# An encoder layer on one core: about 135 stores and loads move from SyncE's DMA queue to GpSimd's, and two gate norms change their chain

## The chip, the cores and the metric

The kernel runs on one core of one Trainium2 chip. The metric is device time in microseconds for one launch, median of several runs. The engines are named as the profile names them: PE (TensorE, matrix products), DVE (VectorE), ACT (ScalarE), POOL (GpSimd) and SP (SyncE, which here issues DMA transfers only). A transfer is issued by an instruction on the queue of one of these engines; it lands later, and whoever reads the data waits for its semaphore. DRAM stands for the chip's main memory.

## The reference, cut to what matters

One layer of a hybrid encoder, in fp32, for 1,024 prompt tokens of one stream and 64 sample tokens of another, model width 1,024:

```python
hn = rmsnorm(h, pre_mix_g)
z, xbc, dt, u_pool = split(hn @ w_in)               # 1,024 -> mixer widths
xbc = silu(causal_conv(xbc));  y, new_ssm = ssd_scan(xbc, softplus(dt))
y = (y + d_skip * xs) * silu(z)
y = grouped_rmsnorm(y, 2 groups) * ssm_norm_g       # the "gate norm"
pool = multiscale_causal_pool(u_pool)               # windows 2, 4, 8, 16
h = h + rmsnorm(concat(y, pool) @ w_out, post_mix_g)         # h1
f = (silu(hn2 @ w_gate) * (hn2 @ w_up)) @ w_down    # hn2 = rmsnorm(h1, pre_ffn_g)
h = h + rmsnorm(f, post_ffn_g)                      # h2
e = (p @ w_ple_proj) * sigmoid(h @ w_ple_gate)
y = h + rmsnorm(e, ple_norm_g)
```

Outputs are y for both groups and the new scan, convolution and pooling states.

## The kernel before

**Tiles.** Features lie on the 128 partitions, tokens along the free axis. The 1,088 tokens are four chunks of 272; the last chunk holds 208 prompt tokens and the 64 sample tokens. An fp32 product is made of three products of a shorter float format: each operand is split into a high half (a cast on ACT) and a low half (a subtraction in the helper `sub`, line 424, on DVE and at some places on POOL), and high x high, high x low and low x high are summed in PSUM.

**Stages.** Input projection and convolution; the scan in nine blocks; pooling; z gate and gate norm; output projection; post-mix norm with the residual x, whose result `h1` is stored to DRAM (`h1_d`); the FFN; and a last stage per chunk. The FFN uses a seven-product scheme over 2 x 2 blocks. It needs sums and differences of blocks, called forms. Forms of the FFN's input (`hq_d`) and of its inner activation (`af_d`) are stored to DRAM as they arise and loaded again later, by `al_...` and `ar_...` tiles, for the down product. The two stages overlap: while the last gate and up products run, the first down products start. Into gaps go the products of `p @ w_ple_proj`, whose result is stored to `e_d`.

**The last stage** (`post_ffn`, `post_ple`). For each chunk and each of four pairs of feature blocks, `two(i)` scales the FFN's result by `post_ffn_g` (ACT, two steps), multiplies it by the norm's factor, which PE has spread over the partitions (DVE, line 2566), adds the residual `h1`, which has been loaded into an `hr` tile (POOL line 2572 or DVE line 2575, by the pair), and splits the sum into the halves of `H2` (ACT line 2580, then `sub`). PE then multiplies by `w_ple_gate` (lines 521 and 504; its weights come as `raw_pg` and are split into `w_pg`, two of the eight low halves on POOL). `e_load` fetches a piece of the projection into an `el` tile. A tile's name in the profile is that of its buffer's first or last user, so an `hr` load can read `sq_f<-h_dram`, and an `el` load `sg<-e_dram`.

**Norm factors** (`rstd_job`, from line 526). PE sums squares over the partitions (line 539), DVE turns the sums into 1/sqrt on a small tile (`t_g` for gate norms), PE spreads it (line 548). There are two ways: ACT's reciprocal square root followed by three DVE steps (lines 582 to 591), open to some names once its table has been loaded, and a chain of nine DVE steps without ACT (lines 553 and 596 to 610).

**What sets the order.** The program is written by a planner, `Layout`. Jobs are generators that ask for an engine and a planned time; the planner keeps a clock for each engine and issues whatever can start first. The orders of PE, DVE, ACT and POOL are then fixed as written. `dma` (line 398) issues on a queue, SP's by default, and counts the same planned time whichever queue it is. Each queue issues in order: an instruction that waits holds what stands behind it. Transfers of a queue take turns on eight semaphores, so each also waits for the one eight before it. In the kernel before, one transfer goes through POOL's queue (the small load of `wdr` at the start) and 510 by SP's; POOL otherwise has 47 counted operations, mostly residual additions and low halves.

Of the kernel before, what the change touches and what calls it, by code (L numbers as in the profile page):

```python
# [7 lines left out]
F32 = mybir.dt.float32  # L8
# [12 lines left out]
CW = 272  # L21
# [320 lines left out]
def trunk(ctx, tc, xT, par, wmix, wdt, poolw, wout, wff, wdn, wpg, wpp, pT, ssm0,  # L342
# [63 lines left out]

    cp = const.tile([P, PWIDTH], F32, name="cp")
    scr = const.tile([P, 2], F32, name="scr")
    tabled, z_left = [False], [4 * NC]
# [115 lines left out]
    def rstd_job(accs, L, D, name, got, fast=False, rest=None, free=nts.give):  # L525
# [53 lines left out]

        if tabled[0] and (name[0] in "gmh" or name == f"f{ORD_E[0]}"):  # L580
            yield ("A", 0.2)
            ac.activation(y, v, AF.Abs_reciprocal_sqrt, scale=2.0 ** -24)
            if name == f"h{ORD_F[-1]}":
                tabled[0] = False
                ac.activation(scr[:, 0:1], ones[:, 0:1], AF.Silu)
            yield ("D", 0.16)
            ve.scalar_tensor_tensor(q, y, -(2.0 ** -37), y, ALU.mult, ALU.mult)
            yield ("D", 0.16, TW)
            ve.tensor_tensor(q, q, v, ALU.mult)
            yield ("D", 0.16, TW)  # L590
            ve.scalar_tensor_tensor(y, q, 1.5 * 2.0 ** -12, y, ALU.add, ALU.mult)
            yield from spread()
            return
# [560 lines left out]
    def ssd(c):  # L1154
# [89 lines left out]
        if c >= 7:  # L1244
            dma(ssm_o[:, c - 7], new, 512)
        if c + 1 < NSSD:
# [7 lines left out]
    def ssd_start():  # L1254
        yield lambda: bool(dt_done)
        spawn(decay(0), 2)
        yield lambda: 7 in conv_done
        yield ("S", 0, 1)
        dma(conv_o, conv_out, 48)
        spawn(ssd(0), 2)  # L1260
# [22 lines left out]
    def pool_post(gi):  # L1283
# [32 lines left out]
        for c, (t0, L) in enumerate(CH):  # L1316
# [15 lines left out]
            if M[c] is None:  # L1332
                yield ("S", 0, 0)
                dma(pool_d[c][:, gi], p_[:, :CH[c][1]], CH[c][1])
                spawn(give_later(nts, 4))
                spilled.append((c, gi))
            else:
                spawn(pool_split(c, gi, p_), 2)
# [3 lines left out]
        if len(pool_n) == 4:  # L1342
            exts.to_pages()
            dma(pool_o, pool_out, 120)

# [147 lines left out]
    def post_mix(c, mf, ss):  # L1493
# [7 lines left out]
        def two(i):  # L1501
# [21 lines left out]
            if XM[i] != "A":  # L1523
                n2.give(xr)
            at = dma(h1_d[c][:, 2 * i:2 * i + 2], v, 2 * L)
            ss2.add(v, lambda: spawn(scale(i, v, at), P_SCL))
# [126 lines left out]
    def qforms():  # L1653
# [20 lines left out]
        def form(f, src):  # L1674
# [7 lines left out]
            def low():  # L1682
# [4 lines left out]
                yield ("S", 0, 0)  # L1687
                Q_AT[f] = dma(hq_d[FORMS.index(f)], pg.bitcast(F32), 4 * CW)

# [404 lines left out]
    def whole_forms(q):  # L2094
# [3 lines left out]
        def store(f, t):  # L2098
            yield ("S", 0, 0)
            at[f] = dma(af_d[j][FORMS.index(f)].rearrange("p (c t) -> p c t", c=2), t, 2 * CW)  # L2100
            A_DONE[j, f] = 2
# [24 lines left out]
    def aforms(q):  # L2126
# [8 lines left out]
        def form(f, t):  # L2135
# [7 lines left out]
            def low():  # L2143
# [5 lines left out]
                for s in range(2):  # L2149
                    dma(dst[:, s, sl], v[:, s, sl].bitcast(F32), q.n * CW)  # L2150
                A_DONE[j, f] = A_DONE.get((j, f), 0) + q.n
# [61 lines left out]
    def proj_ready(c, m):  # L2213
        return lambda: c in p_done and f"pp{m // 4}" in W and len(banks.order) > 1

    def proj_group(c, m):
        def emit():
# [5 lines left out]
            def job():  # L2223
# [5 lines left out]
                yield ("S", 0, 0)  # L2229
                dma(e_d[c][:, m], e_, CW)  # L2230
                spawn(give_later(nts, 4), 5)
# [315 lines left out]
    def post_ffn(c, ss, prio):  # L2547
# [6 lines left out]
        def two(i):  # L2554
            v = fp2(c, i)
            for q in range(2):
                yield ("A", 0.5)
                ac.activation(v[:, q], v[:, q], AF.Identity, scale=pcol("post_ffn_g", 2 * i + q))
            if XF[i] != "A":
                yield n2.ok  # L2560
                hr = n2.take(f"hr{c}_{i}")
                yield ("S", 0, 0)
                at = dma(hr, h1_d[c][:, 2 * i:2 * i + 2], 2 * L)
            yield lambda: bool(flag)
# [103 lines left out]
    def e_load(c, i):  # L2668
        yield n2.ok
        e_ = n2.take(f"el{c}_{i}")  # L2670
        yield ("S", 0, 0)
        EL[c, i] = e_, dma(e_, e_d[c][:, 2 * i:2 * i + 2], 2 * CW)

# [213 lines left out]
```

## Time and profile before

| what | value |
|---|---|
| median of 3 runs | 1199.31 us (1197.8 to 1199.6) |
| the profiled execution | 1199.71 us, its span 1197.9 us |
| granted TensorE clock, mean | 0.995 |
| PE busy | 1182.2 us, 99% |
| DVE busy | 946.3 us, 79% |
| ACT busy | 619.3 us, 52% |
| POOL busy | 59.9 us, 5% |
| SP's queue (q1) | 176.56 MB, 43.7% of the 16 DMA engines |
| GpSimd's queue (q0) | 0.03 MB |

All times inside the execution are microseconds from the start of the span. Busy time of an engine says how much it did, not whether anyone waited for it; the list of waits says what PE stood still for, and the chain of waits names, step by step, what released the next piece of work.

### The profile page before, as it was taken

How to read it: one execution, taken by the hardware profiler on the slowest of the kernel's cores; microseconds unless marked ns; L12 is line 12 of the kernel's file. 1: busy time of each engine (PE TensorE's matmuls, PEld its weight loads, DVE VectorE, ACT ScalarE, POOL GpSimd, SP SyncE). 2: the span in 40 equal slices, each digit the busy share in tenths (PEclk: the TensorE clock that was granted, in tenths of full speed). 3: DMA queues.
4: the chain of work that ended last, by engine and by line, in shares of the span. 5: the costliest groups of instructions: out<-in, count | busy, mean ns of one | idle time of the engine just before them, and what ended most of it. 6: DMA issues, size and time to landing. Idle time of an engine off the chain costs nothing.

```text
span 1197.9 us, 23999 instructions
## 1 busy us (share of the span) xinstructions
PE 1182.2 (99%) x9547; PEld 1166.1 (97%) x9547; DVE 946.3 (79%) x1792; ACT 619.3 (52%) x1278; POOL 59.9 (5%) x48
## 2 busy tenths in 40 slices
PE   9999999999999999999999999999999999999997
PEld 7999999999999999999999999999999999999997
DVE  7697777875788797888888888888788688768855
ACT  7355657965668644444443344334554344347533
POOL 0000000111131000000000000000000000012301
PEclk9999999999999999999999999999999999999998
DMA  7022222143455224536546744677865254144422
GB/s 252 23 75 90 75 79 94 54 135 108 148 181 176 69 100 139 183 120 244 204 160 227 250 145 161 231 248 253 316 207 148 87 191 152 30 146 139 157 66 84
DMA packets 73380, 178.13 MB, mean 149 GB/s; under 512 B 8540, under 2 KB 16548, under 8 KB 73268
## 3 DMA queue, kind: packets, MB, share of 16 engines
q1 hardware_dynamic: 73092, 176.56, 43.7%
q8 instruction: 75, 1.23, 0.4%
q14 instruction: 37, 0.30, 0.1%
q0 software_dynamic: 32, 0.03, 0.0%
q10 hardware_dynamic: 144, 0.00, 0.0%
HBM read 131.50 MB, written 45.07 MB: 147 GB/s over the span
## 4 chain that ended last, share of the span: by engine, by line
PE 65%; DVE 2%; DMA 1%; issue 0%; DVEq 0%; SPq 0%; ACT 0%
PE psall L1921 47%; PE psall L2065 7%; PE psall L504 7%; PE psall L521 2%; DMA al_B<-af_dram 1%; DMA hr<-h_dram 0%; PE psall L539 0%; DVE E L2611 0%; DVE mixf L1550 0%; DVE mixf L1580 0%; DVE h_T L424 0%; PE psall L548 0%; DVE h L424 0%; DVE f L2338 0%; DVE f L2566 0%
## 5 line engine op out<-in xcount | busy, mean ns | idle before, releaser
L504 PE MATMUL psall<-x,w_in 128*128 128x272 f32 x1440 | 193.5, 290 | 0.0
L504 PEld LDWEIGHTS psall<-x,w_in 128*128 128x128 f32 x1440 | 183.9, 188 | 3.3 <-issue 2.8
L1921 PE MATMUL psall<-h_T,w_u_S 128*128 128x272 f32 x792 | 104.4, 288 | 0.0
L1921 PE MATMUL psall<-h_T,w_g_S 128*128 128x272 f32 x792 | 101.6, 288 | 0.2 <-DVE h_T L424 0.2
L1921 PEld LDWEIGHTS psall<-h_T,w_u_S 128*128 128x128 f32 x792 | 101.2, 188 | 0.0
L1921 PE MATMUL psall<-al_T,w_d_S 128*128 128x272 f32 x780 | 100.7, 288 | 0.0
L1921 PEld LDWEIGHTS psall<-h_T,w_g_S 128*128 128x128 f32 x792 | 100.1, 188 | 0.4 <-DVE h_T L424 0.4
L1921 PEld LDWEIGHTS psall<-al_T,w_d_S 128*128 128x128 f32 x780 | 98.9, 188 | 0.0
L504 PE MATMUL psall<-mix,w_out 128*128 128x272 f32 x720 | 93.3, 289 | 0.0
L504 PEld LDWEIGHTS psall<-mix,w_out 128*128 128x128 f32 x720 | 90.9, 188 | 0.0
L2338 DVE TENSOR_TENSOR f<-f,psall 128x544 f32<-128x544 f32 (+1 forms) x96 | 60.4, 636 | 32.7 <-PE psall L1921 32.1
L504 PE MATMUL psall<-h,w_pg 128*128 128x272 f32 x576 | 75.4, 290 | 0.0
L504 PEld LDWEIGHTS psall<-h,w_pg 128*128 128x128 f32 x576 | 73.0, 188 | 0.0
L1921 PE MATMUL psall<-al_B,w_d_A 128*128 128x272 f32 x528 | 71.1, 288 | 1.0 <-DMA al_B<-af_dram 1.0
L1921 PEld LDWEIGHTS psall<-al_B,w_d_A 128*128 128x128 f32 x528 | 68.1, 188 | 1.3 <-DMA al_B<-af_dram 1.3
L1802 ACT CAST w_d_S<-raw_d 128x384 fp32r<-128x384 f32 (+2 forms) x55 | 27.8, 530 | 58.0 <-DVE raw_d L1837 37.8
L424 POOL TENSOR_TENSOR w_pg<-raw_pg,w_pg 128x1024 fp32r<-128x1024 f32 x2 | 5.3, 2630 | 684.7 <-DVE f L2338 684.7
L1921 PE MATMUL psall<-h_B,w_g_A 128*128 128x272 f32 x288 | 38.3, 288 | 0.7 <-DVE sq_m L2082 0.7
L1921 PE MATMUL psall<-h_B,w_u_A 128*128 128x272 f32 x288 | 38.0, 288 | 0.0
L1921 PEld LDWEIGHTS psall<-h_B,w_g_A 128*128 128x128 f32 x288 | 36.9, 188 | 0.9 <-DVE sq_m L2082 0.9
L1921 PE MATMUL psall<-al_T,w_d_A 128*128 128x272 f32 x276 | 37.6, 289 | 0.0
L1921 PEld LDWEIGHTS psall<-h_B,w_u_A 128*128 128x128 f32 x288 | 36.8, 188 | 0.0
(559 smaller groups left out, 2488.1 us busy)
## 6 DMA issues: line engine op xcount, KB each, us to landing
hs_T<-hq_dram SPq DMA_DIRECT2D x28, 544.0 KB, 6.2
hs_B<-hq_dram SPq DMA_DIRECT2D x21, 544.0 KB, 5.7
raw_g<-in_wff_dram SPq DMA_DIRECT2D x22, 512.0 KB, 5.3
raw_u<-in_wff_dram SPq DMA_DIRECT2D x22, 512.0 KB, 4.5
raw_in<-in_wmix_dram SPq DMA_DIRECT2D x15, 512.0 KB, 3.7
af_dram<-sq_m SPq DMA_DIRECT2D x26, 272.0 KB, 5.2
ar_T<-af_dram SPq DMA_DIRECT2D x24, 272.0 KB, 3.4
raw_d<-in_wdn_dram SPq DMA_DIRECT2D x10, 512.0 KB, 4.3
```

Source lines behind the costliest of these rows:

```text
L424: eng.tensor_tensor(lo, src, hi.bitcast(F32), ALU.subtract)
L504: pe.matmul(out, lhsT, rhs, start=i == 0, stop=i == n - 1)
L521: pe.matmul(out, w.v(wi, k), act.v(xi, k, L), start=first and n == 0, stop=not left and n == 2)
L1802: ac.copy(v[:, 0], src)
L1921: pe.matmul(d[:, p - q.ps[0], :], w.v(wi, k), u.b(bf, xi, p, k), start=start and not k and not wi and not xi, stop=k == u.ks - 1 and wi == ...
L2065: pe.matmul(d, w.v(wi, k), b[:, xi, k, :], start=m in (1, 2, 5) and not k and not wi and not xi, stop=k == 1 and wi == 1, skip_group_check ...
L2338: ve.tensor_tensor(v[:, sl], v[:, sl], src[:, pl], ALU.add)
```

## The change

Constants name a queue for each kind of transfer. To GpSimd's queue go the stores of scan, convolution and pooling states (`ST_A`), of pooled pieces that are kept in DRAM (`ST_P`), of the forms (`ST_F`, for `hq_d` and `af_d`), and in the last stage the loads of the residual (`LD_H`) and of the projection (`LD_E`). Stores of `h1` and of the projection stay on SP (`ST_H`, `ST_E`). Gate norms lose ACT's way, so that all four chunks use the nine steps; of the four, the first two did so before, because the table was not loaded yet. Two more edits stand in the diff: the residual's load in `two` is issued ahead of the two scalings instead of behind them, and a projection group may start when one PSUM bank is free, where two were asked for. One line is inserted, so lines from 408 on are one higher in the changed kernel.

```diff
@@ -407,2 +407,3 @@
     cp = const.tile([P, PWIDTH], F32, name="cp")
+    ST_A, ST_P, ST_H, ST_F, ST_E, LD_H, LD_E = gp, gp, sy, gp, sy, gp, gp
     scr = const.tile([P, 2], F32, name="scr")
@@ -579,3 +580,3 @@
 
-        if tabled[0] and (name[0] in "gmh" or name == f"f{ORD_E[0]}"):
+        if tabled[0] and (name[0] in "mh" or name == f"f{ORD_E[0]}"):
             yield ("A", 0.2)
@@ -1244,3 +1245,3 @@
         if c >= 7:
-            dma(ssm_o[:, c - 7], new, 512)
+            dma(ssm_o[:, c - 7], new, 512, ST_A)
         if c + 1 < NSSD:
@@ -1258,3 +1259,3 @@
         yield ("S", 0, 1)
-        dma(conv_o, conv_out, 48)
+        dma(conv_o, conv_out, 48, ST_A)
         spawn(ssd(0), 2)
@@ -1333,3 +1334,3 @@
                 yield ("S", 0, 0)
-                dma(pool_d[c][:, gi], p_[:, :CH[c][1]], CH[c][1])
+                dma(pool_d[c][:, gi], p_[:, :CH[c][1]], CH[c][1], ST_P)
                 spawn(give_later(nts, 4))
@@ -1343,3 +1344,3 @@
             exts.to_pages()
-            dma(pool_o, pool_out, 120)
+            dma(pool_o, pool_out, 120, ST_A)
 
@@ -1524,3 +1525,3 @@
                 n2.give(xr)
-            at = dma(h1_d[c][:, 2 * i:2 * i + 2], v, 2 * L)
+            at = dma(h1_d[c][:, 2 * i:2 * i + 2], v, 2 * L, ST_H)
             ss2.add(v, lambda: spawn(scale(i, v, at), P_SCL))
@@ -1687,3 +1688,3 @@
                 yield ("S", 0, 0)
-                Q_AT[f] = dma(hq_d[FORMS.index(f)], pg.bitcast(F32), 4 * CW)
+                Q_AT[f] = dma(hq_d[FORMS.index(f)], pg.bitcast(F32), 4 * CW, ST_F)
 
@@ -2099,3 +2100,3 @@
             yield ("S", 0, 0)
-            at[f] = dma(af_d[j][FORMS.index(f)].rearrange("p (c t) -> p c t", c=2), t, 2 * CW)
+            at[f] = dma(af_d[j][FORMS.index(f)].rearrange("p (c t) -> p c t", c=2), t, 2 * CW, ST_F)
             A_DONE[j, f] = 2
@@ -2149,3 +2150,3 @@
                 for s in range(2):
-                    dma(dst[:, s, sl], v[:, s, sl].bitcast(F32), q.n * CW)
+                    dma(dst[:, s, sl], v[:, s, sl].bitcast(F32), q.n * CW, ST_F)
                 A_DONE[j, f] = A_DONE.get((j, f), 0) + q.n
@@ -2213,3 +2214,3 @@
     def proj_ready(c, m):
-        return lambda: c in p_done and f"pp{m // 4}" in W and len(banks.order) > 1
+        return lambda: c in p_done and f"pp{m // 4}" in W and banks.ok()
 
@@ -2229,3 +2230,3 @@
                 yield ("S", 0, 0)
-                dma(e_d[c][:, m], e_, CW)
+                dma(e_d[c][:, m], e_, CW, ST_E)
                 spawn(give_later(nts, 4), 5)
@@ -2555,5 +2556,2 @@
             v = fp2(c, i)
-            for q in range(2):
-                yield ("A", 0.5)
-                ac.activation(v[:, q], v[:, q], AF.Identity, scale=pcol("post_ffn_g", 2 * i + q))
             if XF[i] != "A":
@@ -2562,3 +2560,6 @@
                 yield ("S", 0, 0)
-                at = dma(hr, h1_d[c][:, 2 * i:2 * i + 2], 2 * L)
+                at = dma(hr, h1_d[c][:, 2 * i:2 * i + 2], 2 * L, LD_H)
+            for q in range(2):
+                yield ("A", 0.5)
+                ac.activation(v[:, q], v[:, q], AF.Identity, scale=pcol("post_ffn_g", 2 * i + q))
             yield lambda: bool(flag)
@@ -2671,3 +2672,3 @@
         yield ("S", 0, 0)
-        EL[c, i] = e_, dma(e_, e_d[c][:, 2 * i:2 * i + 2], 2 * CW)
+        EL[c, i] = e_, dma(e_, e_d[c][:, 2 * i:2 * i + 2], 2 * CW, LD_E)
 
```

SP has 322 rows where it had 457, POOL 169 where it had 52; PE has 4,579 for 4,582. Three places follow.

**The down product's first loads, on SP.** Before, with the stores of forms (`af_dram<-`) among the loads of forms (`al_...`):

```order
L399 DMA raw_d_0_1_9853<-in_wdn_dram 128x512
L399 DMA al_B_9891<-af_dram 128x1088
L399 DMA hs_T_9902<-hq_dram 128x1088
L399 DMA af_dram<-n_g_21_5485 128x544
L399 DMA al_B_9944<-af_dram 128x1088
L399 DMA al_B_9947<-af_dram 128x1088
L399 DMA al_T_9949<-af_dram 128x1088
L399 DMA al_T_9959<-af_dram 128x1088
L399 DMA af_dram<-p_3802 128x544
L399 DMA al_T_9968<-af_dram 128x1088
```

and with the change:

```order
L399 DMA raw_d_0_1_9861<-in_wdn_dram 128x512
L399 DMA al_B_9899<-af_dram 128x1088
L399 DMA hs_T_9910<-hq_dram 128x1088
L399 DMA al_B_9952<-af_dram 128x1088
L399 DMA al_B_9955<-af_dram 128x1088
L399 DMA al_T_9957<-af_dram 128x1088
L399 DMA al_T_9967<-af_dram 128x1088
L399 DMA al_T_9976<-af_dram 128x1088
L399 DMA al_T_10020<-af_dram 128x1088
```

The stores have left the row of loads; the two loads of `al_B` now stand straight behind the load of `hs_T`.

**The entry of the last stage.** SP before, with the four residual loads (`h_0_dram`) behind the loads of `raw_pg`:

```order
L399 DMA raw_pg_12495<-in_wpg_dram 128x1024
L399 DMA raw_pg_12555<-in_wpg_dram 128x1024
L399 DMA raw_pg_12598<-in_wpg_dram 128x1024
L399 DMA raw_pg_12633<-in_wpg_dram 128x1024
L399 DMA sq_f_12205<-h_0_dram 128x544
L399 DMA hr_1_12659<-h_0_dram 128x544 x2
L399 DMA sq_f_12610<-h_0_dram 128x544
L399 DMA raw_pg_12731<-in_wpg_dram 128x1024
L399 DMA raw_pg_12814<-in_wpg_dram 128x1024
```

and POOL with the change:

```order
L399 DMA af_dram<-n_g_21_5491 128x544
L399 DMA af_dram<-p_3810 128x544
L399 DMA af_dram<-sq_m_3274 128x544
L425 TENSOR_TENSOR w_pg_12615<-raw_pg_12566,w_pg_12614 128x1024
L399 DMA sq_f_12216<-h_0_dram 128x544
L399 DMA hr_1_12653<-h_0_dram 128x544 x2
L399 DMA hr_3_12668<-h_0_dram 128x544
L2573 TENSOR_TENSOR f_0_10455<-f_0_10455,sq_f_12216 128x2x272
L425 TENSOR_TENSOR w_pg_12626<-raw_pg_12609,w_pg_12625 128x1024
L2573 TENSOR_TENSOR f_0_10140<-f_0_10140,hr_1_12653 128x2x272
L399 DMA hr_3_12668<-e_dram 128x544
```

The four loads now stand behind the last store of forms and one low half of `w_pg`, and ahead of POOL's first addition; a second low half stands between the two additions.

**The gate norm of chunk 2 on DVE, then PE.** DVE before:

```order
L424 TENSOR_TENSOR w_out_3185<-raw_out_3182,w_out_3184 128x1024
L553 TENSOR_SCALAR t_g_3224<-psall 68x8
L424 TENSOR_TENSOR w_out_3209<-raw_out_3206,w_out_3208 128x1024
L587 SCALAR_TENSOR_TENSOR t_g_3224<-t_g_3224 68x8
L589 TENSOR_TENSOR t_g_3224<-t_g_3224 68x8
L591 SCALAR_TENSOR_TENSOR t_g_3224<-t_g_3224 68x8
L1416 SCALAR_TENSOR_TENSOR xs<-xs,cp,psall 128x272 x3
```

and with the change:

```order
L425 TENSOR_TENSOR w_out_3185<-raw_out_3182,w_out_3184 128x1024
L554 TENSOR_SCALAR t_g_3224<-psall 68x8
L597 TENSOR_SCALAR t_g_3224<-t_g_3224 68x8
L599 TENSOR_TENSOR t_g_3224<-t_g_3224 68x8
L601 TENSOR_TENSOR t_g_3224<-t_g_3224 68x8
L425 TENSOR_TENSOR w_out_3209<-raw_out_3206,w_out_3208 128x1024
L603 SCALAR_TENSOR_TENSOR t_g_3224<-t_g_3224 68x8
L605 SCALAR_TENSOR_TENSOR t_g_3224<-t_g_3224 68x8
L607 TENSOR_TENSOR t_g_3224<-t_g_3224 68x8
L609 SCALAR_TENSOR_TENSOR t_g_3224<-t_g_3224 68x8
L611 SCALAR_TENSOR_TENSOR t_g_3224<-t_g_3224 68x8
L1406 TENSOR_TENSOR acc_g_3_3246<-acc_g_3_3246,sq_g_3_3247 128x272
```

Three of the nine steps now stand ahead of a low half of `w_out`, five behind it, and an addition of squares for chunk 3 follows at once. PE before, around the spread of that factor:

```order
L504 MATMUL psall<-mix_00_2389,w_out_3169 128x272 x4
L504 MATMUL psall<-mix_01_2390,w_out_3169 128x272
L548 MATMUL psall<-cp,t_g_3224 128x68 x8
L504 MATMUL psall<-mix_01_2390,w_out_3169 128x272 x3
L504 MATMUL psall<-mix_00_2389,w_out_3184 128x272 x4
```

and with the change:

```order
L505 MATMUL psall<-mix_00_2389,w_out_3169 128x272 x4
L505 MATMUL psall<-mix_01_2390,w_out_3169 128x272 x4
L505 MATMUL psall<-mix_00_2389,w_out_3184 128x272 x3
L549 MATMUL psall<-cp,t_g_3224 128x68 x8
L505 MATMUL psall<-mix_00_2389,w_out_3184 128x272
```

The spread stands six products later. Chunk 3's sum and spread with the change:

```order
L540 MATMUL psall<-cp,acc_g_3_3312 68x1 x4
L505 MATMUL psall<-mix_00_2636,w_out_3072 128x272 x2
L505 MATMUL psall<-mix_01_2637,w_out_3072 128x272 x4
L505 MATMUL psall<-mix_00_2636,w_out_3119 128x272 x4
L505 MATMUL psall<-mix_01_2637,w_out_3119 128x272 x4
L505 MATMUL psall<-mix_10_2638,w_out_3119 128x272 x4
L549 MATMUL psall<-cp,t_g_3368 128x68 x8
```

Between the two stand 18 products; before, there were 15.

## The prediction

> **What bounds the kernel now.** I read the page's busy shares first, then the list of PE's waits, then the chain of waits and the timeline at the places which that list names. Busy share of each engine:
>
> ```profile
> PE 1182.2 (99%) x9547; PEld 1166.1 (97%) x9547; DVE 946.3 (79%) x1792; ACT 619.3 (52%) x1278; POOL 59.9 (5%) x48
> ```
>
> PE is busy for 1182.2 of 1197.9 us, so 15.7 us are all that any order of the work can win. The change leaves the number and the size of the matrix products as they are (eight fillers become four). It can move only waits. PE's waits, in all (us, times, longest):
>
> ```profile
> PE psall L521 <- DVE h L424: 2.6, 1, 2.6
> PE psall L504 <- ACT e L2227: 1.4, 1, 1.4
> PE psall L867 <- DVE wz L863: 1.2, 1, 1.2
> PE psall L548 <- DVE t_g L591: 1.1, 1, 1.1
> PE psall L548 <- DVE t_e L575: 1.1, 1, 1.1
> PE psall L1921 <- DMA al_B<-af_dram: 1.0, 1, 1.0
> PE psall L2615 <- DVE E L2611: 0.8, 1, 0.8
> PE psall L1921 <- DVE sq_m L2082: 0.7, 1, 0.7
> ```
>
> Each happens once. Three of them lie where the change works: 2.6 at the entry of the last stage, 1.1 at a gate norm, and 1.0 at a load of the down product. The start (wz, 1.2) and the tail (t_e, E) keep their instructions. POOL is busy 5% of the span, so its queue has room, and the question is how soon it issues and how long its transfers take.
>
> **The change part by part.** *The price of a GpSimd DMA.* The trace of before has a single one, the small load of `wdr` at the start (ns of one issue, then us from issue to landing). Below it are two issues of SP, of 544 KB each and of 272 KB:
>
> ```profile
> L399 POOL DMA_DIRECT2D wdr<-in_wdt_dram x1: 676/676/676, 1.2 to 1.2; - x1
> DMA to landing us min/median/max: 3.4/3.4/3.4
> ...
> 836.05 0.89 SPq L399 DMA_DIRECT2D al_B<-af_dram  x2
> ...
> 1178.00 0.33 SPq L399 DMA_DIRECT2D el<-e_dram  x1
> ```
>
> It carries 32 KB, while most of the moved transfers carry 272 KB. As a lower bound for issue to landing I take its 3.4 us, and as an upper bound the 5.04 us of the `hr` load in the next fence, which is the same tile by SP's queue. For the issue I take 0.68 us, since on SP twice the bytes cost little more to issue (0.89 / 2 = 0.45 us against 0.33). An issue twice as long would put the second `hr` load 1.4 us later; that end goes to the slow rival.
>
> *Entry of the last stage (LD_H, and the load taken ahead of the two scalings in `two`).* The chain of waits (start, us, what), then four rows of the timeline:
>
> ```profile
> 1072.87 5.04 DMA hr<-h_dram
> ...
> 1078.00 0.93 DVE f L2575
> 1078.93 0.69 DVE f L2338 x2
> 1079.63 0.63 DVE f L2566
> 1080.26 0.70 DVE f L2338 x2
> 1080.95 0.63 DVE f L2566
> 1081.58 1.48 DVE h L424
> ...
> 1083.11 7.68 PE psall L521 x47
> ```
>
> ```profile
> 1066.16 5.61 SPq L399 DMA_DIRECT2D raw_pg<-in_wpg_dram  x2
> 1069.02 2.39 POOL L424 TENSOR_TENSOR w_pg<-raw_pg,w_pg 128x1024 fp32r<-128x1024 f32 x1 [684.74 <-DVE f L2338]
> 1071.89 0.92 SPq L399 DMA_DIRECT2D sq_f<-h_dram  x1
> 1086.65 0.71 DVE L424 TENSOR_TENSOR h<-f,h 128x544 fp32r<-128x544 f32 x1
> ```
>
> The residual for the second pair of feature blocks lands at 1077.91, DVE adds it at 1078.00, and works off its queue until the first low half of H2 is there and PE starts at 1083.11. The first SP load here left at 1071.89, because on SP it stands behind loads of `raw_pg`, the last of which was issued at 1066.16 + 5.61 = 1071.77. In the changed order the four `hr` loads stand on POOL behind one `w_pg` low half, which ends at 1069.02 + 2.39 = 1071.41. The second one then issues at 1071.41 + 0.68 = 1072.1 and lands between 1072.1 + 3.4 = 1075.5 and 1072.1 + 5.04 = 1077.1, which is 0.8 to 2.4 us sooner. DVE's order behind that add grows by one eviction: 2.65 us of the chain (0.69 + 0.63 + 0.70 + 0.63) become 3.0. From the start of the add to PE it is then 0.71 + 3.0 + 0.71 = 4.4 us at best, both additions being as fast as the last row, and 0.93 + 3.0 + 1.48 = 5.4 us as slow as before. PE starts between 1075.5 + 4.4 = 1079.9 and 1077.1 + 5.4 = 1082.5, where before it was 1083.11. That is a gain of 0.6 to 3.2 us. I take 1.3, under the middle, because the last evictions also need PE's last FFN product. If the transfer takes longer than 1083.11 - 5.4 - 1072.1 = 5.6 us, this turns into a loss, one for one. What is queued on POOL behind the four issues is the addition for block pair 0, then another `w_pg` low half, 2.39 us by the row above, and the addition for pair 2, whose result DVE wants third.
>
> *Stores of forms (ST_F).* The timeline at the load that PE waits for, and the tile's landing times:
>
> ```profile
> 829.16 3.17 PE L1921 MATMUL psall<-h_T,w_u_S 128*128 128x272 f32 x24
> 829.80 0.44 SPq L399 DMA_DIRECT2D hs_T<-hq_dram  x1
> 834.89 0.72 DVE L2105 TENSOR_TENSOR n_g<-n_g,xr 128x544 f32<-128x544 f32 x1
> 835.64 0.32 SPq L399 DMA_DIRECT2D af_dram<-n_g  x1
> 842.36 1.02 PE L1921 MATMUL psall<-al_B,w_d_A 128*128 128x272 f32 x6 [1.05 <-DMA al_B<-af_dram]
> DMA to landing us min/median/max: 6.3/7.3/8.4
> ```
>
> SP has issued a form at 829.80 and then holds at the store of `n_g` until DVE is done at 835.61; the load of `al_B` stands behind it and leaves at 836.05, although the page that it fills was set free by the 24 products which end at 829.16 + 3.17 = 832.33. In the changed order that store is POOL's. The load then leaves at about 832.4 and lands by 832.4 + 6.3 to 8.4 = 838.7 to 840.8, ahead of 842.36 - 1.05 = 841.31, at which PE wants it. The whole 1.0 us goes. The price is at least zero here, unless a store on POOL is late and a later load into the same tile holds SP.
>
> *The other moved stores* (states, convolution and pooling results, pooled pieces) have nothing in PE's list of waits that stands behind them. They cost POOL 17 issues of 0.68 us each, ahead of GpSimd additions that are needed later. I put them at nothing. If that cover were gone, an addition of the mix would come one issue later, 0.7 us.
>
> *Gate norms back to nine steps.* Only chunks 2 and 3 change, since the earlier ones took that path already. The timeline for chunk 2:
>
> ```profile
> 267.33 2.81 PE L504 MATMUL psall<-mix,w_out 128*128 128x272 f32 x21
> 268.65 0.15 DVE L553 TENSOR_SCALAR t_g<-psall 68x8 f32<-68x8 f32 x1
> 269.47 1.23 DVE L424 TENSOR_TENSOR w_out<-raw_out,w_out 128x1024 fp32r<-128x1024 f32 x1 [0.67 <-ACT w_out L471]
> 270.61 0.16 DVE L587 SCALAR_TENSOR_TENSOR t_g<-t_g 68x8 f32<-68x8 f32 x1
> 271.00 0.16 DVE L591 SCALAR_TENSOR_TENSOR t_g<-t_g 68x8 f32<-68x8 f32 x1
> 271.22 0.69 PE L548 MATMUL psall<-cp,t_g 68*128 68x68 f32 x8 [1.08 <-DVE t_g L591]
> ```
>
> Steps follow each other at (271.00 - 270.61) / 2 = 0.195 us. In the changed order three steps stand ahead of the `w_out` low half, in the idle 0.67 us there (three take 0.59), and five behind it. Its end does not move, so the fifth step starts at 270.61 + 4 x 0.195 = 271.39, and PE's spread can start 0.22 later at 271.61, where before it was 271.22. PE, however, has six more products ahead of it, 6 x 2.81 / 21 = 0.80 us, and comes there at 267.33 + 2.81 + 0.80 = 270.94. The wait is 0.67 instead of 1.08: a gain of 0.4. For chunk 3 the sums and the spread move ahead together and keep 18 products between them, 18 x 0.134 = 2.4 us, against ten steps of 0.195 and one hop of 0.22, so 2.2 us. That costs nothing, though with little to spare. The bounds for both together are a gain of 1.1 and a loss of 0.6.
>
> *Projection loads (LD_E) and the test for a bank.* The thinnest place is the last chunk's last `el`; the timeline where it is used, and where PE takes what DVE makes of it:
>
> ```profile
> 1183.59 0.44 DVE L2734 TENSOR_TENSOR E<-el,sq 128x272 f32<-128x272 f32 x1 [0.60 <-ACT sq L2732]
> 1185.01 0.44 DVE L685 TENSOR_TENSOR el<-el 128x272 f32<-128x272 f32 x1
> 1186.89 0.60 PE L539 MATMUL psall<-cp,el 128*68 128x1 f32 x8
> ```
>
> Before, it was issued at 1178.00 (above). Issued on POOL then and landing 3.4 to 5.04 us later, it is there by 1183.1, before 1183.59. Behind that, PE takes DVE's result 1186.89 - 1185.45 = 1.4 us after it is there, so a landing up to 7.0 us after the issue costs nothing. I take zero. Asking for one free bank instead of two moves a few rows of PE and no wait that I can see. The 1.4 us behind ACT's `e` stays.
>
> **Sum.** 1.3 + 1.0 + 0.4 = 2.7 us. The profiled execution took 1199.71 us (span 1197.9) and would take 1197.0. It lies 0.4 above the median of the runs, 1199.31, from which the same sum gives **1196.6**. The ends of the three terms are 3.2 + 1.0 + 1.1 = 5.3 gained, and 0.6 + 0 - 0.6, nothing.
>
> **The rivals.** *GpSimd's transfers are slow* (slower). If a 272 KB transfer of that queue takes 9 us from issue to landing, the entry loses 9 - 5.6 = 3.4 us and the tail 9 - 7.0 = 2.0. With 1.4 gained elsewhere this is 4.0 us, so 1203.3. It decides from 7 us on, where the entry's loss has used up that 1.4. For it speaks that the 3.4 us belong to an eighth of the bytes, and that `al_B`, twice the size, took up to 8.4 us by SP's queue; against it, that `hr` took 5.04 by SP while the same DMA engines were busy with `raw_pg`.
>
> The Trainium skill has a rule for this side, in "SBUF — State Buffer", its box on the "DVE blocks DMA" trap: descriptors of a GpSimd DMA are written by GpSimd's own cores, which are locked out while DVE runs a two-port perf-mode operation, such as an fp32 copy. By that rule transfers beside DVE's 79% would be late, and the slow rival's sum would hold. The large DVE rows shown here are TENSOR_TENSOR, not copies, and no run so far shows a GpSimd DMA beside a busy DVE.
>
> *Only the issuer changes, and the waits stay* (no change). The stall at the entry is DVE's own queue as much as the load: from 1078.00 to PE's start DVE is busy throughout, and it has one more eviction there now. If the add comes earlier but the last evictions still wait for PE's last product, the entry gives 0.6. If another load then takes `al_B`'s place, the rest is the 0.4 of the gate norm: 1.0 us, 1198.3. "DMA: Bandwidth & Descriptors" of the Trainium skill, section "Issuing engines are not separate DMA queues", says that several issuers save only sequencer time, which speaks for this one. The 5.4 us for which SP stood behind `n_g` (830.24 to 835.64) is time in order, not time of issue, and speaks against it.
>
> *SP is relieved everywhere* (a larger gain). With about 135 transfers fewer on SP, forms and weights arrive earlier all over the FFN. If the waits on `sq_m` (0.7) and `e` (1.4) go as well, and the entry gives its 3.2, the sum is 3.2 + 1.0 + 0.4 + 2.1 = 6.7 us, 1192.6. Against it: those two wait for DVE and ACT, not for a load.
>
> **How the numbers follow.** Forecast 0.46, slow transfers 0.22, waits stay 0.20, larger gain 0.12. About 0.2% (2.4 us) is what a measurement of this kernel can tell from no change, so the border of faster is 1196.9 and that of slower 1201.7. The forecast's own range, 1194.0 to 1199.3, lies on both sides of 1196.9: 0.26 of its 0.46 is faster, 0.20 is no change. With the larger gain, faster is 0.38. With the waits that stay and a slow case that just crosses 7 us (0.03), no change is 0.43. Slower is 0.19. The range of 8 in 10 is 1192.6 to 1203.3: from the larger gain to the slow rival.
>
> **What would show it.** Right: PE's list without `al_B`; at the entry a wait of about 1.3 us in place of 2.6, with an `hr` landing before DVE's add; `t_g` at about 0.7 and at the nine-step line. Wrong: GpSimd landings above 7 us with the releaser of DVE's add or of `E` being a DMA; GpSimd issues longer than 0.7 us each so that `hr` leaves after 1073; a new wait in the FFN on a tile whose store is still in POOL's queue. The forecast as a whole fails if the sum of PE's waits goes down by less than 1 us or by more than 5.

## The result, and the profile after

| | before | after |
|---|---|---|
| median of 22 runs each (lowest to highest), us | 1199.18 (1197.15 to 1202.46) | 1202.47 (1197.81 to 1204.60) |
| ratio, with its 95% interval | 1 | 1.0025 [1.0016, 1.0034] |
| profiled execution, us (span) | 1199.71 (1197.9) | 1204.60 (1202.8) |

The changed kernel is about 3 us slower, where 2.7 us were forecast as a gain. Its profiled execution is the slowest of its 22, so that a part of what this one profile shows does not stand in the median. Which part, the experiments must tell. The page of the changed kernel, busy shares, then two rows of its DMA queues (packets, MB, share):

```profile
PE 1183.1 (98%) x9539; PEld 1166.7 (97%) x9539; DVE 950.2 (79%) x1802; ACT 619.0 (51%) x1276; POOL 134.3 (11%) x195
...
q1 hardware_dynamic: 51924, 135.98, 33.8%
q0 software_dynamic: 11728, 40.62, 9.2%
```

The move took place: 40.62 MB go by GpSimd's queue, and POOL counts 195 instructions where it had 48. The 147 added are the moved transfers; the 135 of the title are rows of the written order, in which equal neighbours stand as one. PE does the same work, but for eight filler products, and waits more. Its waits (us, times, longest):

```profile
PE psall L1922 <- DVE f L2339: 4.6, 1, 4.6
PE psall L1922 <- DMA al_B<-af_dram: 2.1, 1, 2.1
PE psall L505 <- ACT e L2228: 1.4, 1, 1.4
PE psall L549 <- DVE t_g L611: 0.4, 1, 0.4
```

The gate norm's wait fell from 1.1 to 0.4. The wait on `al_B` did not go, it doubled in this profile. At the entry of the last stage the wait of 2.6 on `h` is gone, and one of 4.6 on an eviction has come.

**The entry.** The chain of waits of the changed kernel (start, us, what), then rows of its timeline at that place:

```profile
1075.36 5.69 DMA hr<-h_dram
1081.14 2.56 DVE f L2576
1083.70 0.36 DVE f L2339
1084.10 4.24 PE psall L1922 x21
1088.72 0.73 DVE h L425
1089.49 6.16 PE psall L522 x47
```

```profile
1072.47 2.39 POOL L425 TENSOR_TENSOR w_pg<-raw_pg,w_pg 128x1024 fp32r<-128x1024 f32 x1 [172.38 <-ACT w_pg L472]
1075.36 1.60 POOL L399 DMA_DIRECT2D hr<-h_dram  x3
1077.60 0.43 DVE L2339 TENSOR_TENSOR f<-f,psall 128x272 f32<-128x272 f32 x1
1080.78 2.33 POOL L425 TENSOR_TENSOR w_pg<-raw_pg,w_pg 128x1024 fp32r<-128x1024 f32 x1
1081.14 2.56 DVE L2576 TENSOR_TENSOR f<-f,hr 128x544 f32<-128x544 f32 x1 [3.11 <-DMA hr<-h_dram]
1084.10 1.73 PE L1922 MATMUL psall<-al_T,w_d_A 128*128 128x272 f32 x6 [4.62 <-DVE f L2339]
```

DVE is through with what stands ahead of the residual's addition at 1078.03 and then stands still for 3.11 us, until `hr` lands at 1081.05. The addition takes 2.56 us, beside POOL's low half of `w_pg`, which runs to 1083.11. The eviction behind it (an eviction takes a result out of a PSUM bank) frees the bank that PE's last 21 products of the FFN need. PE thus stops in front of those products. Before, it had them behind it, and stopped at the first product of the last stage.

**The load of `al_B`.** The timeline of the changed kernel, SP and POOL ahead of the wait:

```profile
820.24 0.38 SPq L399 DMA_DIRECT2D raw_d<-in_wdn_dram  x1
820.49 0.55 POOL L399 DMA_DIRECT2D af_dram<-p  x1 [5.83 <-DVE p L2106]
826.08 0.32 SPq L399 DMA_DIRECT2D p<-af_dram  x1
826.49 0.86 SPq L399 DMA_DIRECT2D al_T<-af_dram  x2
833.00 1.32 SPq L399 DMA_DIRECT2D al_B<-af_dram  x2
844.26 1.38 PE L1922 MATMUL psall<-al_B,w_d_A 128*128 128x272 f32 x6 [2.15 <-DMA al_B<-af_dram]
```

The issue left at 833.00, where it had been 836.05 before. But it takes 11.2 us to land, and before that SP had stood from 820.62 to 826.08 at the reload of `p`, which needs POOL's store of `p`.

**The clock.** Stretches of PE's time (stretch, length, PE busy with products, granted clock, DMA share, GB/s), of the changed kernel behind its two waits, and then of the kernel before behind the one on `h`:

```profile
844.20:847.00 2.80, 2.74 (x13) 0.59 1.02 420
847.00:850.00 3.00, 3.00 (x22) 0.81 1.02 407
1084.00:1086.00 2.00, 1.90 (x8) 0.50 0.00 0
```

```profile
1083.10:1085.00 1.90, 1.89 (x12) 0.76 0.98 369
1085.00:1088.00 3.00, 3.00 (x16) 0.59 0.71 259
```

Behind each of these waits PE runs on at a lowered clock for some us. The 47 products of the last stage that took 7.68 us before take 6.16 in the chain above, because there the fall has passed by then. That is 1.5 us of clock in the kernel before, on top of its wait of 2.6.

So the 4.9 us between the two profiled spans divide up, by the time at which PE comes to the same product: 0.8 ahead of the down product (829.93 against 829.16 at 24 products of `w_u_S`), 2.6 at `al_B` (1.1 more wait, 1.5 of clock behind it), and 1.4 at the entry, where the kernel before also pays for a fall of the clock.

### The profile page after: what moved, and what is told of

Its sections match the earlier page's. It is cut to its first block, busy times and chain, and to the rows that moved or that the text cites. A ratio compares the mean times of both kernels' runs of the same rounds, so it can differ in the third digit from the quotient of the medians.

```text
span 1202.8 us, 24024 instructions
## 1 busy us (share of the span) xinstructions
PE 1183.1 (98%) x9539; PEld 1166.7 (97%) x9539; DVE 950.2 (79%) x1802; ACT 619.0 (51%) x1276; POOL 134.3 (11%) x195
## 3 DMA queue, kind: packets, MB, share of 16 engines
q0 software_dynamic: 11728, 40.62, 9.2%
## 4 chain that ended last, share of the span: by engine, by line
PE 85%; issue 8%; DMA 3%; DVE 2%; ACT 1%; POOL 1%; DVEq 0%; POOLq 0%; ACTq 0%; SPq 0%
PE psall L1922 40%; PE psall L505 29%; PE psall L2066 7%; PE psall L522 3%; DMA al_B<-af_dram 1%; PE psall L540 1%; DMA af_dram<-a_B 1%; POOL af_dram L399 1%; PE psall L1238 1%; PE psall L1209 1%; PE psall L1203 1%; PE psall L549 0%; DMA hr<-h_dram 0%; PE psall L1324 0%; DMA raw_out<-in_wout_dram 0%
## 5 line engine op out<-in xcount | busy, mean ns | idle before, releaser
L1922 PEld LDWEIGHTS psall<-al_T,w_d_A 128*128 128x128 f32 x276 | 36.3, 191 | 5.0 <-DVE f L2339 4.8
```

Source lines behind the costliest of these rows:

```text
L1922: pe.matmul(d[:, p - q.ps[0], :], w.v(wi, k), u.b(bf, xi, p, k), start=start and not k and not wi and not xi, stop=k == u.ks - 1 and wi == ...
```

## The experiments

In the expectations A is the theory that the stores of forms cost the time (by `al_B` and the clock behind its wait), B that the loads of the residual come late on GpSimd's queue at the entry, C that the planner's other order costs it on whatever queue, E that the projection loads do, F that transfers of GpSimd's queue take longer in themselves. Every kernel was timed in five rounds. Medians stand beside the kernel before in the same rounds: 1198.82 for e1 to e4, 1198.02 for e5 to e8, 1198.97 for e9 to e12. These three differ by up to 1 us, so ratios of different sets of rounds can be compared to about that.

**e1_all_sp**: the changed order with all transfers on SP.

```diff
-    ST_A, ST_P, ST_H, ST_F, ST_E, LD_H, LD_E = gp, gp, sy, gp, sy, gp, gp
+    ST_A, ST_P, ST_H, ST_F, ST_E, LD_H, LD_E = sy, sy, sy, sy, sy, sy, sy
```

> The changed kernel with all seven constants set to SP's queue: the planner's order with its nine-step gate norms, the earlier residual load and the one-bank test stays, no transfer moves. Theory A (forms): the loss sits where SP reloads a form whose store is on POOL, in the trace of after a wait of 2.15 us on al_B at 844.26 plus a granted clock of 0.59 to 0.81 behind it, 2.8 us in all. Then this kernel loses none of that and keeps the gate norm's gain of 0.4 to 0.7: 1198 to 1199. Theory B (entry): the loss sits at the entry of the last stage, where POOL's hr loads leave 3.4 us later than worked out, 1.4 us: also 1198 to 1199.5 here. Theory C (order): the planner's new order of DVE, ACT and PE costs the 3.3 us whichever queue is used: 1202 to 1203.

Measured 1197.64, ratio 0.9991 [0.9982, 1.0000]. The order alone costs nothing, C falls, and the queues cost about 0.0034 x 1199 = 4.1 us. Its timeline at the entry, and its wait there:

```profile
1069.13 0.80 SPq L399 DMA_DIRECT2D hr<-h_dram  x2
1072.40 0.38 SPq L399 DMA_DIRECT2D sq_f<-h_dram  x1
1074.96 0.72 DVE L2576 TENSOR_TENSOR f<-f,hr 128x544 f32<-128x544 f32 x1
```

```profile
PE psall L522 <- DVE h L425: 1.8, 2, 1.6
```

On SP, whose order is not fixed as written, the residuals of pairs 1 and 2 leave first, and that of pair 0 (`sq_f`), whose buffer comes free later, leaves behind them. On POOL it leaves ahead of them. The 6 us between 1069.13 here and 1075.36 in the change hold the 3 us by which the change already lagged; about 3 are the place in the queue.

**e2_queues_only**: the kernel before, with the queues alone changed (gate norm, bank test and the place of the load as before).

```diff
-        if tabled[0] and (name[0] in "mh" or name == f"f{ORD_E[0]}"):
+        if tabled[0] and (name[0] in "gmh" or name == f"f{ORD_E[0]}"):
...
-        return lambda: c in p_done and f"pp{m // 4}" in W and banks.ok()
+        return lambda: c in p_done and f"pp{m // 4}" in W and len(banks.order) > 1
...
+            for q in range(2):
+                yield ("A", 0.5)
+                ac.activation(v[:, q], v[:, q], AF.Identity, scale=pcol("post_ffn_g", 2 * i + q))
             if XF[i] != "A":
```

> The kernel before with the queue constants of the change alone; gate norms, the place of the residual's load and the two-bank test as before. Theory A: al_B waits 2 us or more and the clock falls behind it, 1202 to 1203.5, since the gate norm's gain is missing too. Theory B: here the hr loads are issued behind the scalings again, so the entry is as late or later, 1201 to 1202. Theory C: 1199 to 1199.5, no loss.

Measured 1200.21, ratio 1.0006 [0.9995, 1.0017]; the wait on `h` is 3.3. Theory B had expected 1201 to 1202, a miss: the queues without the early load cost no more than a measurement can tell, so it takes both.

**e3_forms_sp**: the change with the forms' stores on SP (the line that goes is e1's, here and below).

```diff
+    ST_A, ST_P, ST_H, ST_F, ST_E, LD_H, LD_E = gp, gp, sy, sy, sy, gp, gp
```

> The changed kernel with the stores of forms (ST_F) back on SP, all else as in the change. Theory A: the al_B wait is 1.0 us as before with no fall of the clock behind it; 2.8 of the 3.3 us come back, 1199.5 to 1200. Theory B: nothing comes back at al_B that counts, 1201.5 to 1202.5. Theory C: 1202 to 1203.

Measured 1201.63, ratio 1.0028 [1.0018, 1.0037]. The `al_B` wait is down to 0.3, yet the loss is all there: A falls, as the cause of what stands in the median. In its timeline:

```profile
1077.39 2.34 POOL L425 TENSOR_TENSOR w_pg<-raw_pg,w_pg 128x1024 fp32r<-128x1024 f32 x1
1078.10 2.22 DVE L2576 TENSOR_TENSOR f<-f,hr 128x544 f32<-128x544 f32 x1 [2.95 <-DMA hr<-h_dram]
```

```profile
PE psall L1922 <- DVE f L2339: 4.1, 1, 4.1
```

The entry is that of the change: DVE waits 2.95 us for the load, its addition ends 0.6 us after POOL's low half (1080.32 against 1079.73), and PE waits 4.1. Against e1, PE is 0.1 us behind ahead of the entry (at the sums of squares, 1070.17 against 1070.07) and 3.7 behind it (1092.45 against 1088.73). Of this, 4.1 - 1.6 = 2.5 are longer wait, and the rest is clock: PE's last 21 products of the FFN take 4.42 us here, and 2.92 in e7, where the wait ahead of them is 0.5 and the clock full.

**e4_loads_sp** and **e5_ldh_sp**: the change with both kinds of loads on SP, and with the residual's alone.

```diff
+    ST_A, ST_P, ST_H, ST_F, ST_E, LD_H, LD_E = gp, gp, sy, gp, sy, sy, sy
```

> The changed kernel with the last stage's residual and projection loads (LD_H, LD_E) back on SP, stores as in the change. Theory A: al_B still waits 2 us and the loss stays but for the entry's 1.4 us: 1201 to 1202. Theory B: most of the loss is gone, 1199 to 1200. Theory C: 1202 to 1203.

```diff
+    ST_A, ST_P, ST_H, ST_F, ST_E, LD_H, LD_E = gp, gp, sy, gp, sy, sy, gp
```

> The changed kernel with the residual loads alone (LD_H) back on SP; projection loads and stores stay on POOL. Theory B, made sharper by the runs so far: the hr loads stand on POOL behind a w_pg low half of 2.39 us, leave at 1071.8 or later where SP issued them at 1068.6, and DVE's add, which waits for them, stands ahead of an eviction that PE's last FFN products need. Then all of the loss is in LD_H: 1198.0 to 1199.2, no wait of PE on DVE's L2339. Theory E: the projection loads (LD_E) carry part of it, since they share POOL with the additions of the last stage: 1200 to 1202.

Measured 1198.54, 1.0002 [0.9993, 1.0010], and 1198.77, 1.0012 [1.0002, 1.0022]. The waits on `h` are 1.5 and 1.7, as in e1. The residual's loads carry the loss (B). The projection loads add nothing that shows: the two medians lie 0.2 us apart, though the ratios, each against its own rounds, leave up to 2 us open.

**e6_low_dve** and **e7_low_dve_sp**: `LOW_G` names the pieces of `w_pg` whose low half POOL computes. Emptied, DVE does them, so that POOL's long addition stands neither ahead of the loads nor beside the addition of the residual; in the change, and in e1.

```diff
-LOW_G = ('pg_3', 'pg_4')
+LOW_G = ()
```

> The changed kernel with no w_pg low half on POOL (both go to DVE, 1.22 us each), so nothing but stores stands ahead of the hr loads there. Theory B: hr leaves about 1070.3 to 1070.9, lands at 1076 to 1077 and the add takes 0.72 instead of 2.2 to 2.6 us, since POOL runs nothing beside it; PE's wait on L2339 falls from 4.1 to 4.6 to between 1 and 2.5 us: 1199 to 1200.5. Theory F: it is the GpSimd queue's own transfer time (5.7 to 6.5 us here against 3.1 on SP at that place), not the place in the order: the wait stays above 3.5 us, 1201 to 1202.5.

> The same without POOL's low halves, and all seven constants on SP: the control for the run before. If DVE has room for two more low halves at the entry, 1197 to 1198.5, as with the low halves on POOL (1197.64); if the two low halves of 1.22 us on DVE delay the first low half of H2, 1199 to 1200. The distance between this run and the one before is the price of the GpSimd loads without a low half ahead of them: 0 to 1 us by theory B's main part, 3 us by theory F.

Measured 1202.69, 1.0046 [1.0034, 1.0058], and 1198.78, 1.0009 [1.0001, 1.0018]. That was a miss: 3.9 us lie between the two (e6 has six runs) without POOL's low halves, so these are not the cause by themselves. The timeline of e6, then a stretch of it, then the first two rows of e7's timeline:

```profile
1071.84 0.54 POOL L399 DMA_DIRECT2D sq_f<-h_dram  x1 [174.21 <-DVE t_f L588]
1072.63 1.67 POOL L399 DMA_DIRECT2D hr<-h_dram  x3 [0.24 <-issue]
1077.15 1.27 DVE L2576 TENSOR_TENSOR f<-f,hr 128x544 f32<-128x544 f32 x1 [1.59 <-DMA hr<-h_dram]
```

```profile
1079.60:1083.00 3.40, 3.40 (x18) 0.53 0.41 154
```

```profile
1069.18 0.80 SPq L399 DMA_DIRECT2D hr<-h_dram  x2
1070.76 0.32 SPq L399 DMA_DIRECT2D sq_f<-h_dram  x1
```

With the low half gone, POOL's queue waits for the buffer of pair 0 instead (174.21 us idle, until DVE's `t_f`), and `hr` still leaves 3.4 us later than on SP. DVE waits for it again, 1.59 us, and PE's wait of 1.8 is followed by a clock of 0.53. That wait is inside theory B's range, the time is above F's. Two more waits follow in e6 (1.4 on ACT's `h`, 1.2 on DVE's), so that PE waits 4.4 at the entry in all, against 2.8 in e7 (1.5, 0.8 and 0.5).

**e8_late_load**: the change with the load behind the two scalings again.

```diff
             v = fp2(c, i)
+            for q in range(2):
+                yield ("A", 0.5)
+                ac.activation(v[:, q], v[:, q], AF.Identity, scale=pcol("post_ffn_g", 2 * i + q))
             if XF[i] != "A":
```

> The changed kernel with the residual's load again behind the two scalings in two(i), still on POOL. The planner then places DVE's add one eviction later, behind the one that PE's last products need; POOL's order at that place is the same. Theory B with the order as its second half: no wait of PE on L2339, the wait on h is 3 to 3.5 us as with the queues alone (3.3), 1199.5 to 1200.5. If the order does not matter and the late landing alone sets PE's start: 1201.5 to 1202.5.

Measured 1198.02, ratio 1.0002 [0.9993, 1.0010]. The early load is the other half of the cause. Its timeline:

```profile
1077.40 1.10 DVE L2576 TENSOR_TENSOR f<-f,hr 128x544 f32<-128x544 f32 x1 [1.20 <-DMA hr<-h_dram]
1082.70 6.16 PE L522 MATMUL psall<-h,w_pg 128*128 128x272 f32 x47 [1.47 <-DVE h L425]
```

The load still leaves late (1072.56, and 1069.13 in e1) and DVE waits 1.20 for it, but the planner leaves the eviction ahead of the addition. So PE has its last products and waits only 1.47, without a fall of the clock. Part of the smaller wait is a sooner landing, 4.75 us here against 5.69.

**e9_gate_only**: the kernel before with the gate norms' path alone.

```diff
-        if tabled[0] and (name[0] in "gmh" or name == f"f{ORD_E[0]}"):
+        if tabled[0] and (name[0] in "mh" or name == f"f{ORD_E[0]}"):
```

> The kernel before with gate norms on the nine steps, nothing else. By the prediction's term the wait on t_g of chunk 2 falls from 1.1 to about 0.7 us and chunk 3 shows none: 0.4 us less than before, ratio 0.9997, inside what can be told. A rival for it: chunk 3's sum and spread, which come earlier, wait instead, 0.3 to 1 us slower.

Measured 1199.07, 0.9995 [0.9985, 1.0004]. The waits on `t_g` are 0.7 + 0.2, against 1.1 + 0.2. A gain of 0.4 us fits in the interval, and so does none.

**e10_forms_only**: the changed order, of the queues the forms' alone on POOL.

```diff
+    ST_A, ST_P, ST_H, ST_F, ST_E, LD_H, LD_E = sy, sy, sy, gp, sy, sy, sy
```

> The changed order with ST_F alone on POOL and every other transfer on SP. Against the all-SP kernel (1197.64) this prices the forms' stores. Theory A in what is left of it: SP's reload of a form waits on a store that POOL issued later and that lands after 5 us, al_B waits 0.6 to 1 us where all-SP showed 0.3, and in some executions 2 us with a fall of the clock: 1198 to 1199.5. If the stores cost nothing: 1197 to 1198.

Measured 1198.07, 0.9990 [0.9982, 0.9999], beside e1's 0.9991. Landing times of the tile `al_B` between 815 and 860 us (lowest, median, highest), of the changed kernel, of e1, and of e10:

```profile
DMA to landing us min/median/max: 9.3/11.0/12.2
```

```profile
DMA to landing us min/median/max: 5.6/6.7/7.9
```

```profile
DMA to landing us min/median/max: 8.7/10.7/11.3
```

With the forms on POOL the loads of `al_B` take 2 to 4 us longer to land, in all eight kernels that have them there (medians 9.8 to 11.0, against 6.7 to 7.7 in the six others). PE's wait on them was 0.5 to 1.1 in seven of the eight, and 0.3 to 1.4 in the six others, so the longer landing is mostly hidden. The 2.1 in the profile of the change is the exception, and belongs to the slowest of its runs.

**e11_hr12_sp**: the change with the residuals of pairs 1 and 2 alone on SP.

```diff
-                at = dma(hr, h1_d[c][:, 2 * i:2 * i + 2], 2 * L, LD_H)
+                at = dma(hr, h1_d[c][:, 2 * i:2 * i + 2], 2 * L, sy if i in (1, 2) else LD_H)
```

> The changed kernel with two of the four residual loads of each chunk (pairs 1 and 2) on SP and the other two on POOL, all else as in the change. On POOL the load of pair 0 comes first and waits for its buffer to be free and for a w_pg low half; pair 1, whose sum DVE forms first, stands behind it. On SP pair 1's load left at 1068.6 to 1069.2. If this place in POOL's order is the cause, PE's wait on L2339 is gone and the time is that of LD_H on SP, 1198 to 1199; if GpSimd loads of the last stage cost in another way, 1200.5 to 1202.

Measured 1198.28, 0.9990 [0.9982, 0.9999]. Two transfers of 272 KB per chunk take the whole loss back, with all others where the change put them. Rows of its timeline:

```profile
1069.88 0.80 SPq L399 DMA_DIRECT2D hr<-h_dram  x2
1075.71 0.72 DVE L2576 TENSOR_TENSOR f<-f,hr 128x544 f32<-128x544 f32 x1
1082.60 5.09 PE L522 MATMUL psall<-h,w_pg 128*128 128x272 f32 x36 [1.69 <-DVE h L425]
```

On POOL these two stand behind a low half of `w_pg` and behind pair 0's load; e6 shows that the latter alone makes them late. That place is worth 3.2 us (they leave at 1072.31 in e3, and at 1069.13 in e1). The landing adds 1.8, 5.7 against 3.9. That POOL's transfers take longer in themselves (F) does not follow from it: leaving at about the same moment (1072.1 to 1072.9), the load took 5.04 us by SP in the kernel before and 4.43 (e6), 4.75 (e8), 5.70 (e3) and 6.45 (e2) by POOL. No run puts the two loads first on POOL, which would part the place from the queue altogether.

**e12_two_only**: the kernel before with the load ahead of the scalings, on SP.

```diff
+            if XF[i] != "A":
+                yield n2.ok
+                hr = n2.take(f"hr{c}_{i}")
+                yield ("S", 0, 0)
+                at = dma(hr, h1_d[c][:, 2 * i:2 * i + 2], 2 * L)
             for q in range(2):
```

> The kernel before with the residual's load ahead of the scalings, on SP, nothing else. The planner then places DVE's add of pair 1 as in the change, but the load leaves at about 1068.6 to 1069.2 and lands before 1073. The wait at the entry falls from 2.6 to 1.6 us, no wait on L2339: about 1 us less than before, ratio 0.9988 to 0.9994. If the new place of the add harms by itself: slower than before by 1 us or more.

Measured 1196.83, 0.9983 [0.9974, 0.9992], the best of all. Its timeline, and the clock behind its wait:

```profile
1073.43 0.72 DVE L2575 TENSOR_TENSOR f<-f,hr 128x544 f32<-128x544 f32 x1
1080.90 5.09 PE L521 MATMUL psall<-h,w_pg 128*128 128x272 f32 x36 [1.83 <-DVE h L424]
```

```profile
1080.90:1083.00 2.10, 2.05 (x14) 1.00 0.81 254
```

The addition comes without a wait and in 0.72 us. PE starts the stage 2.2 us sooner than before (1083.11), and at full clock; 0.7 of that is a shorter wait on `al_B` in this profile (0.3).

## Why the prediction was wrong, point by point

By the prediction's own sign the forecast failed as a whole: the sum of PE's waits did not fall by 1 us or more; as the list of waits has them, it rose from 10.3 to 12.8 us.

**The entry, forecast as 1.3 gained, is the step that failed.** The issue was right: 1075.36, less the 3.45 us by which POOL's low half ahead of it already lagged (1072.47 against 1069.02), is 1071.9, against 1072.1. The landing was not: 5.69 us, where the bounds were 3.4 and 5.04, so that `hr` came at 1077.6 in the time of the kernel before, 0.3 us sooner than its 1077.91, and not 0.8 to 2.4. It also passed the 5.6 us from which the working let the gain turn into a loss, but by that sum the loss would have been 0.1.

What failed is the path behind it. From the start of the addition to PE's 47 products the sum had 4.4 to 5.4 us; it was 1089.49 - 1081.14 = 8.35. Two sizes in it were wrong, and one term was missing. The addition was priced at 0.71 to 0.93 and took 2.56 beside POOL's `w_pg` low half, which the prediction named as queued there, but not as running at that moment. The added eviction was priced at 0.35 us of DVE's queue. Its price is that PE's last 21 products need its bank, so they move behind the load and the addition: 4.24 us of PE that the sum did not have in the chain, 2.92 by their length in e7, the rest lowered clock. And a wait was priced at its own length only, without the clock that falls behind it.

The term itself is sound if the load leaves in time: e12, on SP, gains 2 us (0.0017 x 1199, by its interval 1 to 3).

**The forms, forecast as 1.0 gained, gave nothing.** The earlier issue came as worked out (833.00 less 0.77 is 832.2, against 832.4). The landing of 6.3 to 8.4 us did not carry over to it. SP had waited 5.5 us at a reload for a store that is now on the other queue, and the loads behind it then left in a bunch. That the bunch is what stretches the landing was read from the trace and not tried by itself. The case that the prediction set apart, a late store on POOL that holds SP at a reload, is what happened. In the median it costs nothing that shows (e10 against e1, to about 1 us).

**The gate norm, forecast as 0.4 gained**, went from 1.08 to 0.41 us of wait, where the working left 0.67; in e9 and e1 it is 0.7. As time it can't be told from none (e9).

**Nothing for the projection loads and the other stores** stands, within what e4 and e5 leave open; e11, which has the other stores on POOL, stands at e1's ratio. The price of an issue on POOL, 0.68 us, was 0.54:

```profile
L399 POOL DMA_DIRECT2D hr<-h_dram x3: 536/536/543, 1075.4 to 1076.4; - x3
```

**The rivals.** The slow one was on the right side and within 1 us of the result (1203.3), but that is luck: it put the decision at a landing of 7 us, and no `hr` of the changed kernel took over 6.1 at the entry. That the waits stay was half true: the wait at the entry changed its place and grew. That SP is relieved everywhere did not come. The wide range, 1192.6 to 1203.3, held the time; the forecast's own, 1194.0 to 1199.3, did not.

**What stays open.** How much of e6's loss is the queue's order and how much its own clock was not separated. The clock also moves the whole kernel, and here the runs on record tell more than the one profile of each kernel: the 94 runs of the kernel before beside the experiments have a median of 1197.6 us where their mean granted clock is 0.997 or more (30 runs), and of 1199.5 where it is 0.995 or less (34 runs). What decides in which runs it falls is not known.

## What to carry to other kernels

When a load moves to another queue, list what stands ahead of it there in program order, with the buffer that each entry waits for; a load that could leave ahead of an earlier one on the old queue may not be able to on the new one. When a planner orders the work by a cost that is the same for every queue, an earlier load also moves what waits for it ahead of other work on its engine, so price the whole queue behind the wait, and above all the evictions whose banks the matmuls need. Where a wait of PE reaches about 2 us, add some 1.5 us for the clock behind it, which is what it cost in this kernel.

## What the runs showed of the hardware

**The clock falls behind short waits.** Behind waits of 2.15, 2.64 and 4.62 us the granted clock was 0.59, 0.76 and then 0.59, and 0.50. Behind 1.80 (e6) it was 0.53 and behind 1.83 (e10) 0.58, but behind the 1.83 of e12 it was 1.00, and so also behind 1.74 (e5) and 1.59 (e1). The row of e10:

```profile
1082.20:1085.00 2.80, 2.80 (x14) 0.58 0.08 31
```

In e7 the clock fell to 0.59 behind waits of 1.55 and 0.37 close together. So between about 1.5 and 1.9 us it goes either way in these profiles. The Trainium skill, "TensorE: Matmul & The Clock Gate", section "Part 1: The HAM clock gate (the "warmup" mystery)", has the clock halve after at least one idle window of some 3.4 us. Its windows run freely, which fits that two equal waits end differently; that 1.8 to 2.6 us suffice, here on an engine that is otherwise busy, differs from its figure, and the measurement decides.

**An addition of DVE waits out an operation of POOL.** The same addition of 128x544 takes 0.72 us alone (e1, e12), and 2.22 (e3) and 2.56 (the change) beside POOL's low half, and both times ends 0.6 us after POOL's operation does. The 0.93 of the kernel before and the 1.27 of e6 also end 0.6 us after an operation of POOL. The Trainium skill, "SBUF — State Buffer", section "SBUF: two separate sides", has the port pair that the two engines share as an exclusive lock for a whole instruction, against a DVE operation with two inputs in SBUF. These rows agree with it.

**No large delay of GpSimd's transfers beside a busy DVE was seen.** The stores of forms, with DVE 79% busy over the span, landed in medians of 3.4 to 5.7 us by POOL, where by SP it had been 2.1 to 5.2 before. The loads at the entry do not decide it: `hr` landed in 5.7 to 6.1 us in the change, where by SP it had been 5.0 to 5.3 before, but DVE stood still for 3.11 us of that time, and a load that left about 3 us sooner by SP landed in 3.9 (e1).
